# Two modulation vectors of the second layer, streamed behind the second pair of FFNs instead of the first FFN

## The chip, the cores and the metric

The kernel runs on one core of a Trainium2 chip. A core has a tensor engine for matrix products (TensorE, "PE" in the profile; its weight loads are "PEld"), a vector engine (VectorE, "DVE"), an activation engine (ScalarE, "ACT"), a general engine (GpSimd, "POOL") and a queue that issues transfers (SyncE, "SP"). Each runs its own list of instructions in order, and they wait for one another by semaphores. Sixteen DMA engines carry the transfers between the main memory and the core's own memory. The metric is the device time of one execution in microseconds (us).

## What is computed

Two layers of a diffusion backbone in 32-bit floats, on 256 latent tokens and 256 context tokens of 1024 features. Each layer is an FFN, a mixer (attention in the first layer, a short convolution in the second) and another FFN. Every such part is modulated by vectors that come from the conditioning vector `c`: nine vectors of 1024 numbers for each layer, one product of `silu(c)` with a 1024 x 9216 matrix.

```python
m = (s_c @ ada_w[i] + ada_b[i]).reshape(B, N_MOD, 1, D)
x = half_step_ffn(x, m[:, 0], m[:, 1], m[:, 2], ...)   # shift, scale, gate
hx = modulate(x, m[:, 3], m[:, 4])
x = post_norm_update(x, y_lat, m[:, 5], ...)
x = half_step_ffn(x, m[:, 6], m[:, 7], m[:, 8], ...)
```

An FFN is `(silu(a) * u) @ w_out` with `a, u` the halves of `h @ w_in`, 1024 to 2 x 2816 and 2816 to 1024. The change concerns vectors 2 and 3 of the second layer: the gate of its first FFN and the shift of its convolution.

## The kernel before

**Stages.** The kernel has three phases. The first (`ph0`, 0 to some 400 us) holds the first layer's first FFN for latent and context tokens together. The second (`ph1`, to some 600 us) is the attention. The third (`ph2`) is, from latent tokens alone, the first layer's second FFN, `ffn(..., 0, 1, ...)`, the second layer's first FFN, `ffn(..., 1, 0, ...)`, the convolution mixer and the last FFN. The text calls the first two of these the second pair of FFNs.

**Matrix products.** Every 32-bit factor is split in a high and a low part: ScalarE copies the raw tile to the high part (L216), VectorE subtracts it from the raw tile for the low part (L219). A product is then three matmuls: high by high (L170), low by high (L171), high by low (L173). A weight unit (`wunit`) is 256 rows by 512 columns, one or two loads from SP (L211), two ScalarE instructions and two VectorE instructions (`w1h`, `w1l` for the first matrix, `w2h`, `w2l` for the second). The low parts lie in five buffers and two further ones in `ph2`.

**Ticks.** TensorE's order is written out by hand. After each group of six matmuls the generator yields and `tick()` is called. An FFN in `ph2` has 88 ticks in the first matrix (11 panels, each of four units for two token tiles; panels 0 and 1 together take 16 ticks, each later panel 8) and 44 in the second. The first 5 units of the second matrix are used for the first token tile alone, one per tick; elsewhere a unit serves two ticks.

**Background stream.** Modulation vectors are computed beside the FFNs. `stream` is a generator of single steps. A step loads one slice of 128 rows of `ada_w` for a vector (L316, 128 x 1024, 512 KB, tile `ar`, three buffers) and multiplies an earlier one by its column of `silu(c)` into an accumulator (L305 for the first slice of a vector, L307 for the others; two VectorE instructions of 512 columns each, tile `acc`, two buffers). Eight slices make a vector. `tick()` takes steps at a rate per tick that `set_background` sets; in `ph2` the rate is `ADA_SLOWEST` and the first step comes after a hold of four ticks. The accumulations are queued behind the last gate product (`gate_ins`) and the last weight split.

**How a vector is finished.** The accumulator still holds 128 partial sums for each column. In `ph0` TensorE sums them by 32-row matmuls against `ones` (L342), VectorE adds the bias, and SP stores the rows to the scratch tensor `scr`. In `ph2` (`on_pool`) it is done by `sum_up`: GpSimd waits for the last gate product (`warm`, L350), reduces over the partitions (L356), and adds the result by a DMA of its own to `scr`, where the bias was put at the start of the phase (L357), with a small instruction behind (L359). `sum_up` is called behind the panels `SUM_AT = (2, 4, 6, 7, 8)`, by `need` at the end of the first matrix, and in the convolution. `need(n)` also runs steps at once until `n` vectors are streamed.

**Other work on the same engines.** VectorE and ScalarE also do the gate products (`sil`, L511 and L512), the splits of the transposed gates (`gh`, `gl`, L118 and L119), the layer norms between FFNs (`x`, L446, with `rs` on GpSimd, L435 and L436) and the folded columns of the next modulation (`gcol`, L399 to L402). DMA transposes of the gates (L519) are issued by SP.

Of the kernel before, what the change touches and what calls it, by code (L numbers as in the profile page):

```python
# [19 lines left out]
D = 1024  # L20
# [12 lines left out]
WB = (4, 5, 5)  # L33
PB = {"mm": 3, "at": 3, "tp": 2}
W_EARLY = 40
ADA_SLOW, ADA_FAST, ADA_SLOWEST = 3, 0.6, 0.13
KT_IDLE = 6
BIAS_AT = 24
ADA_LATE = 20
# [31 lines left out]
HOLD = 4  # L71
# [4 lines left out]
def backbone_kernel(  # L76
# [7 lines left out]
    sync = nc.sync  # L84
# [20 lines left out]
    def act(dt=F32, s="a"):  # L105
        return ap.tile([P, 512], dt, tag="act", name=nm(s))
# [10 lines left out]
    def split(src, hi, lo):  # L117
        a = nc.scalar.activation(hi, src, AF.Copy)  # L118
        return a, nc.vector.tensor_tensor(out=lo, in0=src, in1=hi.bitcast(F32), op=ALU.subtract)  # L119
# [20 lines left out]
    def settle():  # L140
        while waiting:
            waiting[0].get()

    def bg_step():
        with tc.high_priority(offset=-ada_late[0]):
            if next(background[0], 0) == 0:
                background[0] = None
# [10 lines left out]
    def set_background(gen, rate, hold=0):  # L158

        background[:] = [gen, rate, -rate * hold]  # L160
# [115 lines left out]
    scr = [tc.dram_tile([2, 9 * D], F32, name=f"scr{i}") for i in range(2)]  # L276
# [72 lines left out]
    def sum_up():  # L349
        mark = [nc.gpsimd.tensor_tensor(out=warm, in0=g[0:1, 0:1], in1=lnc[0:1, 0:1], op=ALU.add)  # L350
                for g in last_gate[:len(sums)]]
        while sums:
            (l, m, v), a = sums.pop(0)
            red = hp.tile([P, D], F32, tag="red", name=nm("red"))
            with queued(mark):
                nc.gpsimd.partition_all_reduce(red, a, P, ReduceOp.add)  # L356
            nc.gpsimd.dma_start(scr[l][v:v + 1, m * D:(m + 1) * D], red[0:1], accum_op=ALU.add)  # L357
            if not sums:
                nc.gpsimd.tensor_tensor(out=warm, in0=red[0:1, 0:1], in1=lnc[0:1, 0:1], op=ALU.add)  # L359
# [3 lines left out]
    def need(n):  # L363
        while made[0] < n:
            bg_step()
        sum_up()

    def stream(*groups):
        for g in groups:
            yield from ada(g)  # L370
            made[0] += 1
            if made[0] == ADA_SLOW:
                background[1] = ADA_FAST
# [101 lines left out]
    def lead_in(np):  # L475

        r = range(KU)
        o = [(0, 0, u) for u in r] + [(0, 1, u) for u in r[:2]] + [(1, 0, u) for u in r] + [(1, 1, u) for u in r[:2]]
        o += [(t, 1, u) for u in r[2:] for t in range(2)]
        return o + [(t, p, u) for p in range(2, np) for u in r for t in range(2)]  # L480

    def panels(cols, w, hTs, order, done, s, own=()):


        units, banks = {(0, u): x for u, x in enumerate(own)}, {}
        for t, p, u in order:
            if (p, u) not in units:
                with ExitStack() as st:
                    for i in fence if p == 1 else first_mv if own and p == 0 else ():
                        st.enter_context(tc.issue_after(i))  # L490
                    units[p, u] = wpair(w, u, *cols[p], s)
            if (t, p) not in banks:
                banks[t, p] = mmb(s, t)
            hi, lo = units[p, u]
            mmu(banks[t, p], [(*hsl(hTs[t], UK * u + i), hi[:, i], lo[:, i]) for i in range(UK)], u == 0, u == KU - 1)
            if u == KU - 1:
                done(p, t, banks.pop((t, p)))
            yield
            tick()

    def run(gen):
        for _ in gen:
            pass
# [39 lines left out]
    def order_skew(nu):  # L543

        u = [(n, i) for n in range(2) for i in range(nu)]
        o = []
        for i in range(len(u) + LEAD):
            if i < len(u):
                o.append((0, *u[i]))
            if i >= LEAD:  # L550
                o.append((1, *u[i - LEAD]))
        return o

    def order_last(nu):

        return order_skew(nu)[:-TAIL] + [(1, 1, u, c, c + 256) for c in (0, 256) for u in range(nu - TAIL, nu)]

    def order_late(nu, halved=False):


        e = nu - 1
        banks = ((0, 0), (0, 1), (1, 0))
        o = [(t, n, u) for t, n in banks for u in range(e - 1)] + [(t, n, e - 1) for t, n in banks]
        if halved:
            o += [(t, n, (e, i)) for i in range(UK) for t, n in banks]
        else:
            o += [(t, n, e) for t, n in banks]
        return o + [(1, 1, u) for u in range(nu)]
# [182 lines left out]
    for q, (k0, n) in enumerate(steps):  # L751
        nxt = start_step(*steps[q + 1]) if q < 4 else iter(())
        for g in range(6 * n):
# [7 lines left out]
            else:  # L761
# [3 lines left out]
    sync.dma_start(rope, rope_tab.rearrange("(t p) a b -> p t a b", p=P))  # L765
    w_early[0] = W_EARLY
    set_background(stream([(0, 2, 0), (0, 2, 1)], [(0, 3, 0), (0, 3, 1)], [(0, 4, 0), (0, 4, 1)],
                          [(0, 5, 0), (0, 6, 0)], [(0, 7, 0), (0, 8, 0)], [(1, 0, 0), (1, 1, 0)],
                          [(1, 2, 0), (1, 3, 0)]), 0.45)
    ada_late[0] = 0  # L770
    stats, gates, hTs = {}, [], {}
    GB = None
# [94 lines left out]
    def lhs_T(tl):  # L867
        def f(k, t):
            s = (k % 2) * 256 + t * P
            g = tl[k // 2]  # L870
            hi, lo = g.get() if isinstance(g, Late) else g
            return hi[:, s:s + P], lo[:, s:s + P]
        return f

    def ffn(hTs, later, l, j, i, gm, nxt, own=(), vectors=0):
        def finish(p, ps):
            hi, lo = act(F32R, "gh"), act(F32R, "gl")
            split(ps, hi, lo)
            return hi, lo

        done, gT = gated(AF.Silu, finish, "gT", BY_DMA)

        def done2(p, t, bk):
            done(p, t, bk)
            if t == 1:
                if p == 1:
                    later()
                if p in SUM_AT:
                    sum_up()

        run(panels([(p * 256, FF + p * 256) for p in range(NP)], ffn_w_in[l, j], hTs, lead_in(NP), done2, "w1", own))
        need(vectors)
        g, hTs, later = sub_end(ffn_w_out[l, j], lhs_T(gT), 2 * NP, l, i, gm, 0.5, nxt, "w2",
                                order_skew(NP) if nxt else order_last(NP))
        run(g)
        return hTs, later
# [263 lines left out]
    hTs, later = box  # L1160
    phase = tc.tile_pool(name="ph2", bufs=1)
    hp = phase.__enter__()
    on_pool[0] = True
    sync.dma_start(scr[1][0, 4 * D:9 * D].rearrange("(a b) -> a b", a=16), ada_b[1, 4 * D:9 * D].rearrange("(a b) -> a b", a=16))
    ext[0] = 2

    v0 = made[0]
    set_background(stream(*([(1, m, 0)] for m in range(4, 8))), ADA_SLOWEST, HOLD)
    hTs, later = ffn(hTs, later, 0, 1, 2, 8, (1, 0), own)

    hTs, later = ffn(hTs, later, 1, 0, 0, 2, (1, 3), (), v0 + 1)


    srow = cp.tile([P, P], F32, tag="row", name="srow")
# [33 lines left out]
    def done(p, t, bk):  # L1208
        if p >= 2:
            cdone(p, t, bk)  # L1210
            if t == 1:
                sum_up()
            return
        b = sp.tile([P, 512], F32, tag="s2", bufs=S2, name=nm("bs"))
        nc.scalar.activation(b, bk, AF.Copy)
        bs[p, t] = b
        last_gate[:] = [b]
        if p == t == 1:
            sum_up()
        if t == 1:  # L1220
            for j in range(2):
                def rest(j=j):
                    ps = tpb("bT")
                    for i in range(2):
                        for t in range(2):
                            nc.tensor.transpose(ps[:, i * 256 + t * P:i * 256 + (t + 1) * P],
                                                bs[p, t][:, (2 * j + i) * P:(2 * j + i + 1) * P], ident)
                    b = act(F32, "bT")
                    nc.scalar.activation(b, ps, AF.Copy)
                    return b  # L1230
                bT[2 * p + j] = Late(G_LAG, rest)
            if p == 1:
                later()

    cols = [(0, 256), (512, 768)] + [(D + n * 256, 2 * D + n * 256) for n in range(4)]
    run(panels(cols, w, hTs, lead_in(6), done, "wc"))
    need(v0 + 4)
    g, hTs, later = sub_end(sc_w_out[0], lhs_T(yT), KC, 1, 1, 5, 1.0, (1, 6), "wo", order_late(KU))
    run(g)
    set_background(stream([(1, 8, 0)]), 0.15)  # L1240
    ffn(hTs, later, 1, 1, 2, 8, None, (), v0 + 5)
    settle()
    phase.__exit__(None, None, None)

# [51 lines left out]
```

## Time and profile before

| what | value |
|---|---|
| median of 3 runs | 1245.14 us (1244.8 to 1246.18) |
| the profiled execution, whole | 1246.53 us |
| its span, first to last instruction | 1244.7 us |
| granted TensorE clock | 0.998 of full |
| slices loaded for vectors (`ar` at L316) | 128 of 512 KB |
| accumulations, L305 and L307 | 38 of 482 ns and 266 of 747 ns |
| matmuls against `ones` (L342) | 56 records, 7 groups, 97.7 to 362.2 us |
| all-reduces on GpSimd (L356) | 5 of 6.1 to 6.5 us, 722.2 to 1154.0 us |

A page of the profile gives, for one execution, each engine's busy time and the groups of instructions with their mean duration and the idle time ahead of them. A table by stage gives the busy time of each engine with its count of instructions in a stretch of the span. A timeline gives the instructions of an engine in order, and for the idle time before one, in brackets, what ended it. A name such as `w1l<-w1r,w1h` says what is written and what is read.

### The profile page before, as it was taken

The page shows a single profiled execution, that of the slowest core. Times are in us where ns is not written, and L with a number is a line of the kernel's source. Part 1 is how long each engine was busy: PE and PEld are TensorE (multiplying, and loading weights), DVE is VectorE, ACT ScalarE, POOL GpSimd, SP SyncE. Part 2 cuts the span into 40 slices and gives each one's busy share as a digit, 9 for nine tenths or more (in the row PEclk, how much of TensorE's full clock was granted, in tenths as well). Part 3 has the DMA queues.
Part 4 walks back from the last instruction along what each step waited for, and adds up shares of the span by engine and source line. Part 5 has one row for each costly group of instructions (what it writes and reads, how often), then busy time and mean ns, then how long its engine had stood idle before and what let it go on. Part 6 is the DMA issues. An engine that isn't in the chain of part 4 may idle for free.

```text
span 1244.7 us, 17236 instructions
## 1 busy us (share of the span) xinstructions
PE 1225.9 (98%) x5794; PEld 995.3 (80%) x5794; DVE 965.2 (78%) x1675; ACT 643.7 (52%) x1233; POOL 81.6 (7%) x93
## 2 busy tenths in 40 slices
PE   8999999999999999999999999999999999999997
PEld 5787778778778878777788888888888887888886
DVE  3698987888878867888877677878867798768746
ACT  2433132321325566687777635668645644678631
POOL 0000000000001011120000020020200110000200
PEclk9999999999999999999999999999999999999999
DMA  9986679778852654554899957879886765799851
GB/s 294 305 249 228 177 235 298 259 253 289 285 187 68 179 116 95 121 111 128 264 296 311 269 202 242 231 231 324 246 286 225 220 220 153 204 279 277 245 186 68
DMA packets 232304, 275.67 MB, mean 221 GB/s; under 512 B 59622, under 2 KB 178910, under 8 KB 232216
## 3 DMA queue, kind: packets, MB, share of 16 engines
q1 hardware_dynamic: 232020, 274.54, 73.0%
q8 instruction: 45, 0.74, 0.2%
q14 instruction: 43, 0.35, 0.1%
q0 software_dynamic: 160, 0.02, 0.1%
q10 hardware_dynamic: 36, 0.02, 0.0%
HBM read 265.27 MB, written 2.20 MB: 215 GB/s over the span
## 4 chain that ended last, share of the span: by engine, by line
PE 90%; DVE 4%; DMA 3%; ACT 2%; issue 1%; SPq 0%; POOL 0%; DVEq 0%; ACTq 0%
PE f L729 19%; PE w L170 17%; PE w L171 17%; PE w L173 17%; PE wkv L170 3%; PE wkv L171 2%; PE wkv L173 2%; DMA ar<-in_ada_w_dram 1%; PE wc L170 1%; PE wc L171 1%; PE wc L173 1%; PE S L1026 1%; PE o L1064 1%; PE hT L454 1%; PE PT L1051 1%
## 5 line engine op out<-in xcount | busy, mean ns | idle before, releaser
L219 DVE TENSOR_TENSOR w1l<-w1r,w1h 128x512 fp32r<-128x512 f32 (+1 forms) x352 | 232.0, 704 | 44.5 <-ACT w1h L216 43.6
L216 ACT ACTIVATE w1h<-w1r 128x512 fp32r<-128x512 f32 (+1 forms) x352 | 198.2, 617 | 112.0 <-DMA w1r<-in_ffn_w_in_dram 40.8
L170 PE MATMUL w<-w1h,hTh 128*128 128x512 f32 x528 | 206.3, 391 | 1.2 <-ACT hTh L118 1.2
L171 PE MATMUL w<-w1l,hTh 128*128 128x512 f32 x528 | 205.6, 389 | 0.0
L307 DVE SCALAR_TENSOR_TENSOR acc<-ar,cst,acc 128x512 f32<-128x512 f32 x266 | 186.6, 747 | 12.3 <-DMA ar<-in_ada_w_dram 11.9
L170 PE MATMUL w<-w2h,gh 128*128 128x512 f32 (+1 forms) x446 | 173.3, 389 | 0.0
L171 PE MATMUL w<-w2l,gh 128*128 128x512 f32 (+1 forms) x446 | 172.2, 387 | 0.0
L216 ACT ACTIVATE w2h<-w2r 128x512 fp32r<-128x512 f32 x176 | 101.3, 624 | 135.5 <-PE w L173 95.0
L173 PE MATMUL w<-w1h,hTl 128*128 128x512 f32 x528 | 162.6, 389 | 0.0
L219 DVE TENSOR_TENSOR w2l<-w2r,w2h 128x512 fp32r<-128x512 f32 x176 | 117.7, 710 | 57.6 <-ACT w2h L216 56.7
L173 PE MATMUL w<-w2h,gl 128*128 128x512 f32 (+1 forms) x446 | 136.1, 386 | 0.0
L729 PE MATMUL f<-h0h,w1h 128*128 128x512 f32 x352 | 132.4, 392 | 1.9 <-ACT w1h L216 1.5
L729 PE MATMUL f<-h0l,w1h 128*128 128x512 f32 x352 | 133.0, 391 | 0.0
L729 PE MATMUL f<-h0h,w1l 128*128 128x512 f32 x352 | 132.8, 390 | 0.0
L170 PEld LDWEIGHTS w<-w1h,hTh 128*128 128x128 f32 x528 | 99.1, 188 | 22.5 <-ACT hTh L118 2.1
L173 PEld LDWEIGHTS w<-w1h,hTl 128*128 128x128 f32 x528 | 99.0, 188 | 20.9 <-DVE hTl L119 0.4
L171 PEld LDWEIGHTS w<-w1l,hTh 128*128 128x128 f32 x528 | 99.2, 188 | 20.6 <-DVE w1l L219 0.3
L170 PEld LDWEIGHTS w<-w2h,gh 128*128 128x128 f32 x446 | 83.8, 188 | 19.2 <-issue 1.7
L171 PEld LDWEIGHTS w<-w2l,gh 128*128 128x128 f32 x446 | 83.8, 188 | 16.9 <-DVE w2l L219 0.3
L173 PEld LDWEIGHTS w<-w2h,gl 128*128 128x128 f32 x446 | 83.3, 188 | 17.1
L729 PEld LDWEIGHTS f<-h0h,w1h 128*128 128x128 f32 x352 | 65.7, 188 | 19.5 <-issue 3.4
L729 PEld LDWEIGHTS f<-h0l,w1h 128*128 128x128 f32 x352 | 65.6, 188 | 14.2 <-issue 0.8
(197 smaller groups left out, 1763.6 us busy)
## 6 DMA issues: line engine op xcount, KB each, us to landing
w1r<-in_ffn_w_in_dram SPq DMA_DIRECT2D x340, 256.0 KB
ar<-in_ada_w_dram SPq DMA_DIRECT2D x128, 512.0 KB
w2r<-in_ffn_w_out_dram SPq DMA_DIRECT2D x88, 512.0 KB
ar<-in_ada_w_dram SPq DMA_DIRECT2D x32, 256.0 KB
wkvr<-in_na_w_qkv_dram SPq DMA_DIRECT2D x32, 256.0 KB
wcr<-in_sc_w_in_dram SPq DMA_DIRECT2D x32, 256.0 KB
wqr<-in_na_w_qkv_dram SPq DMA_DIRECT2D x8, 512.0 KB
wor<-in_na_w_out_dram SPq DMA_DIRECT2D x8, 512.0 KB
```

Source lines behind the costliest of these rows:

```text
L170: nc.tensor.matmul(ps, lh, rh, start=first and i == 0, stop=False)
L171: nc.tensor.matmul(ps, lh, rl, start=False, stop=False)
L173: nc.tensor.matmul(ps, ll, rh, start=False, stop=last and i == n - 1)
L216: last_split[:] = [nc.scalar.activation(hi[:, a:a + m // W_HI], raw[:, a:a + m // W_HI], AF.Copy)]
L219: last_lo[:] = [nc.vector.tensor_tensor(out=lo[:, a:b], in0=raw[:, a:b], in1=hi[:, a:b].bitcast(F32), op=ALU.subtract)]
L307: nc.vector.scalar_tensor_tensor(out=a, in0=src, scalar=sc, in1=a, op0=ALU.mult, op1=ALU.add)
L454: nc.tensor.transpose(ps[:, k * P:(k + 1) * P], z[h][:, k * P:(k + 1) * P], ident)
L729: nc.tensor.matmul(ps, w, hT0[k][part == 1], start=(k == part == 0), stop=(k == KC - 1 and part == 1))
L1026: nc.tensor.matmul(banks[i], (qh, ql, qh)[f][ps, qs], (kh, kh, kl)[f][ps, :], start=f == 0, stop=f == 2)
L1051: nc.tensor.transpose(pt[:, k * P:(k + 1) * P], pr[:, k * P:(k + 1) * P], ident)
L1064: nc.tensor.matmul(ps, v[k][:, s], p[:, k], start=k == part == 0, stop=part == 1 and k == 3)
```

## The change

The first stream ends with vectors 0 and 1 of the second layer; vectors 2 and 3 go to the head of the second stream, which so has six vectors instead of four. Its rate goes from 0.13 to 0.21 steps per tick. The bias of seven vectors instead of five is put into `scr` at the start of the phase. The counts that `need` waits for are relative to `v0`, the count of groups streamed earlier, and grow by two for the two vectors more.

```diff
-ADA_SLOW, ADA_FAST, ADA_SLOWEST = 3, 0.6, 0.13
+ADA_SLOW, ADA_FAST, ADA_SLOWEST = 3, 0.6, 0.21
...
-                          [(0, 5, 0), (0, 6, 0)], [(0, 7, 0), (0, 8, 0)], [(1, 0, 0), (1, 1, 0)],
-                          [(1, 2, 0), (1, 3, 0)]), 0.45)
+                          [(0, 5, 0), (0, 6, 0)], [(0, 7, 0), (0, 8, 0)], [(1, 0, 0), (1, 1, 0)]), 0.45)
...
-    sync.dma_start(scr[1][0, 4 * D:9 * D].rearrange("(a b) -> a b", a=16), ada_b[1, 4 * D:9 * D].rearrange("(a b) -> a b", a=16))
+    sync.dma_start(scr[1][0, 2 * D:9 * D].rearrange("(a b) -> a b", a=16), ada_b[1, 2 * D:9 * D].rearrange("(a b) -> a b", a=16))
...
-    set_background(stream(*([(1, m, 0)] for m in range(4, 8))), ADA_SLOWEST, HOLD)
+    set_background(stream(*([(1, m, 0)] for m in range(2, 8))), ADA_SLOWEST, HOLD)
...
-    hTs, later = ffn(hTs, later, 1, 0, 0, 2, (1, 3), (), v0 + 1)
+    hTs, later = ffn(hTs, later, 1, 0, 0, 2, (1, 3), (), v0 + 3)
...
-    need(v0 + 4)
+    need(v0 + 6)
...
-    ffn(hTs, later, 1, 1, 2, 8, None, (), v0 + 5)
+    ffn(hTs, later, 1, 1, 2, 8, None, (), v0 + 7)
```

## The prediction

> **What bounds the kernel now.** I read the page's busy shares first, then the table by stage (busy time and instructions of each engine in a stretch, granted clock, share of the 16 DMA engines, GB/s), since a share over the whole span hides which stage has room.
>
> ```profile
> PE 1225.9 (98%) x5794; PEld 995.3 (80%) x5794; DVE 965.2 (78%) x1675; ACT 643.7 (52%) x1233; POOL 81.6 (7%) x93
> 48.00:362.00 314.00, 314.00 (x1404) 254.24 (x1402) 268.18 (x429) 96.14 (x168) 0.00 (x0) 1.00 0.77 248
> 525.00:600.00 75.00, 71.11 (x400) 55.65 (x401) 63.92 (x135) 59.09 (x128) 11.88 (x16) 1.00 0.54 137
> 600.00:715.00 115.00, 115.00 (x511) 95.06 (x510) 87.06 (x149) 83.52 (x155) 0.00 (x0) 1.00 0.97 284
> 715.00:777.00 62.00, 62.00 (x280) 50.82 (x279) 46.72 (x74) 27.92 (x53) 9.17 (x6) 1.00 0.66 220
> 777.00:898.00 121.00, 120.77 (x538) 99.48 (x537) 98.37 (x157) 86.85 (x160) 16.78 (x9) 1.00 0.91 259
> 898.00:960.00 62.00, 62.00 (x280) 51.12 (x279) 45.06 (x76) 27.69 (x52) 1.30 (x3) 1.00 0.79 259
> 960.00:1055.00 95.00, 93.50 (x435) 76.52 (x433) 80.05 (x139) 52.25 (x103) 10.20 (x8) 1.00 0.63 197
> ```
>
> TensorE bounds every stage. In the first FFN (48 to 362) it is never idle, though VectorE is busy 85% there. In the two FFNs of the change (600 to 960) it is idle for 0.23 us in all. So work taken from VectorE, SP or the DMA engines in the first FFN frees no TensorE time, and work added to the later FFNs costs nothing until a weight comes late. What counts is TensorE's own work that goes, and how far VectorE runs ahead of TensorE where work arrives.
>
> **What is removed.** Two vectors leave the first stream: 16 slices (16 `ar` loads of 512 KB, 32 VectorE instructions), two bias loads, one VectorE add, two stores to `scr`, and four 32-row matmuls against `ones` (L342). Only the matmuls are on TensorE. The last group's eight records stand between two matmul streams:
>
> ```profile
> 361.60 0.39 PE L729 MATMUL f<-h0h,w1l 128*128 128x512 f32 x1
> 361.82 0.39 PE L729 MATMUL f<-h0l,w1h 128*128 128x512 f32 x1
> 362.14 1.06 PE L342 MATMUL ada<-acc,ones 128*32 128x512 f32 x8
> 363.14 0.50 PE L170 MATMUL w<-w2h,gh 128*128 128x512 f32 x1
> ```
>
> From 361.82 to 363.14 are 1.32 us where two neighbouring matmuls are 0.23 apart, so the group costs 1.1 us: **-1.1 us**. The rest lies beside a TensorE without idle time: nothing. The attention stage's 3.9 us of idle time (75 - 71.11) begin some 160 us after the stream's end; I take no gain, and keep 3.9 as the bound of one.
>
> **What is added.** 16 slices more go into the streams behind the second FFN pair, and two more sums on GpSimd. A tick is six matmuls, 1.36 us. Loads come at 0.21 per tick for 0.13, so 0.08 per tick more: 7 in the 88 ticks of the first matrix, 3.5 in the 44 of the second. Step n falls on tick 4 + n/0.21; the accumulation lags one step, so vector j (from 0) is complete at step 8j + 9: ticks 47, 85, 123, 161, 199, 237, where four stood at 73, 135, 196, 258. Sums are taken behind panels 2, 4, 6, 7, 8 and at the end of the first matrix (ticks 24, 40, 56, 64, 72, 88 of an FFN of 132). So vectors 2 to 7 are summed at ticks 56, 88, 156, 172, 204 and in the convolution; before it was 88, 156, 204 and the convolution. **New are tick 56 (first FFN of the pair) and tick 172 (second, behind panel 4).** The second comes 16 ticks behind a sum that exists. `need(v0 + 3)` at tick 220 asks for 40 steps and finds 45, so it forces nothing.
>
> What a sum does to VectorE is in its rows and GpSimd's (start, duration, instruction):
>
> ```profile
> 820.16 0.63 POOL L350 TENSOR_TENSOR warm<-sil,lnc 1x1 f32<-1x1 f32 x1 [38.29 <-DVE sil L512]
> 827.48 6.13 POOL L356 PARTITION_ALL_REDUCE red<-acc  x1 [6.69 <-issue]
> 842.33 0.18 POOL L359 TENSOR_TENSOR warm<-red,lnc 1x1 f32<-1x1 f32 x1 [7.42 <-issue]
> 880.37 0.29 POOL L350 TENSOR_TENSOR warm<-sil,lnc 1x1 f32<-1x1 f32 x1 [37.86 <-DVE sil L512]
> 954.19 0.52 POOL L435 TENSOR_TENSOR rs<-mv,lnc 128x1 f32<-128x1 f32 x1 [50.63 <-DVE mv L433]
> 820.00 1.41 DVE L307 SCALAR_TENSOR_TENSOR acc<-ar,cst,acc 128x512 f32<-128x512 f32 x2
> 824.77 1.29 DVE L219 TENSOR_TENSOR w1l<-w1r,w1h 128x512 fp32r<-128x512 f32 x2
> 827.52 5.63 DVE L219 TENSOR_TENSOR w1l<-w1r,w1h 128x512 fp32r<-128x512 f32 x2 [1.47 <-ACT w1h L216]
> 836.12 1.29 DVE L219 TENSOR_TENSOR w1l<-w1r,w1h 128x512 fp32r<-128x512 f32 x2
> 843.36 0.42 DVE L512 TENSOR_TENSOR sil<-sil,w 128x256 f32<-128x256 f32 x1 [0.97 <-ACT sil L511]
> ```
>
> The pair of `w1l` beside the all-reduce takes 5.63 us where others take 1.29: VectorE is held for **4.3 us**. GpSimd itself is taken for 22 us (820.16 to 842.5); behind the new sum stands `rs` of the layer norm, not wanted before 954, so nothing waits there. With two accumulators, vector 4's first write (tick 166, at the earliest 777 + 34 x 1.36 = 823) waits for the all-reduce of vector 2 to end at 833.6, most of it while VectorE is held anyway; the rest is in the upper bound below. How much it can spare is read from the instructions on `w1l`, counted from 766, ahead of this FFN's first (columns: TensorE, weight loads, VectorE). A unit is two on VectorE and four on TensorE.
>
> ```profile
> 766.00:827.00 61.00, 28.02 (x72) 13.52 (x72) 26.94 (x42) 1.00 0.81 236
> 766.00:833.00 67.00, 31.45 (x81) 15.30 (x82) 32.41 (x44) 1.00 0.81 239
> 766.00:838.00 72.00, 34.24 (x88) 16.63 (x89) 34.10 (x47) 1.00 0.79 232
> 766.00:850.00 84.00, 41.24 (x106) 19.91 (x106) 41.52 (x59) 1.00 0.84 239
> 766.00:882.00 116.00, 59.49 (x153) 28.86 (x154) 59.00 (x86) 1.00 0.92 263
> ```
>
> At 827 VectorE has begun 21 units, TensorE 18: 3 ahead, 8 us. At 838 TensorE is through 22, and unit 23 (the pair after the 44 begun by 833, done at 836.12 + 1.29 = 837.4) is there 0.6 us ahead. So **one sum eats the lead down to 0.6 us**, and it comes back to 4.75 units (43 - 38.25) by 882: some 3.5 units of 2.72 us in 44 us, 0.22 us per us.
>
> A further slice costs VectorE two L307, 1.33 us back to back. 0.08 per tick make 0.078 us per us, and the regained lead falls to 0.14 if nothing hides them. These rows of the stage (busy, mean ns, idle before it) say what could:
>
> ```profile
> L219 DVE TENSOR_TENSOR w1l<-w1r,w1h 128x512 fp32r<-128x512 f32 x80 | 55.4, 739 | 9.5 <-ACT w1h L216 9.4
> L512 DVE TENSOR_TENSOR sil<-sil,w 128x256 f32<-128x256 f32 x20 | 8.2, 417 | 8.0 <-ACT sil L511 8.0
> ```
>
> The 9.5 us ahead of `w1l` can take work in; the 8.0 ahead of `sil` hardly, since ScalarE waits there for VectorE's `sil` in turn. I take half as hidden: 0.18 us per us. The terms:
> - Sum at tick 156: the half-hidden slices since 785 (2.5 of 1.33 us) take 1.7 from the 0.6 left: stall **1.0** (0 to 2.7).
> - Sum at tick 172: its first instruction waits for panel 4's gate (843.36) and, behind the other on GpSimd, for 842.33; the all-reduce follows 7.3 us later, near 851. The lead has regained 0.18 x 13 = 2.3. It takes 4.3 by the row above, some 6 by the fall of the lead at the first sum: stall **3.0** (0.7 to 4.2).
> - Sum at tick 204: 32 us give back 5.8, it takes 4.3 to 6, and the second matrix's first five units are used at one per tick: **1.0** (0 to 4).
> - Sums in the pair's first FFN: at tick 56 the lead stands; the one at tick 88 meets a smaller lead, see below: **0.4** (0 to 3).
> - Turn from FFN to FFN, below: **0.6** (0 to 1.3).
>
> ```profile
> 782.52 1.11 PE L454 MATMUL hT<-ident,x 128*128 128x128 f32 x8 [0.23 <-DVE x L446]
> 775.47 1.33 DVE acc L307 x2
> 722.19 6.13 POOL L356 PARTITION_ALL_REDUCE red<-acc  x1 [5.74 <-issue]
> 723.90 2.85 DVE L400 SCALAR_TENSOR_TENSOR gcol<-gcol 128x8 f32<-128x8 f32 x1
> 650.00:675.00 25.00, 25.00 (x112) 20.70 (x111) 20.07 (x35) 20.69 (x39) 0.00 (x0) 1.00 1.13 327
> ```
>
> At the turn TensorE already waits 0.23 us, and the chain of waits runs through an accumulation (775.47); 16 us of it hold 0.9 more, at 1.33 each at most. At 722 the sum holds VectorE (2.85 us for a 128x8 instruction) while TensorE uses a unit per tick; before, VectorE was as far ahead as its buffers allow. The loads: 7 more `ar` are 3.7 MB on 32.7 (115 us at 284 GB/s), 316 GB/s, under the 327 seen from 650 to 675. SP issues them in one queue with the weights, so a late `ar` buffer also holds weights; I put that into the high end.
>
> [...]
>
> **The sum.** 1.0 + 3.0 + 1.0 + 0.4 + 0.6 - 1.1 = +4.9 us. The profiled execution took 1246.53 (span 1244.7, 1.8 around it), so it would take 1251.4; it lies 1.4 above the median of 1245.14, so the forecast is **1250.0**.
>
> **The rivals.**
> 1. Not slower: the idle 9.5 us hide all slices, and stalls are no more than the lead. It decides at the second of the two close sums: lead over 5 us at 850 (before: 2.5 to 3 units, 59/2 - 106/4, so it needs nearly what was there plus what the sum at 156 no longer takes). Then 1245.1 - 1.1 = 1244, up to 1247 with the turn's wait. For it: no stall in either FFN today. Against: 0.6 us left after a single sum.
> 2. Nothing is hidden, and the loads run late: the upper ends, 2.7 + 4.2 + 4 + 3 + 1.3 - 1.1 = +14, some 1259, or 1254 and over. For it: DMA share 0.97 and 0.91; against: VectorE's idle time.
> 3. Faster: the attention stage gains from the emptied first FFN, or the turn into the convolution from a stream that ends 21 ticks earlier (237 for 258). Bounds: 3.9 and 1.5 (95 - 93.50); with the 1.1, 1239 at best, likelier 1242. Against: TensorE is busy all of 898 to 960.
> 4. That the change doesn't stream the vectors where it says: the counts above leave no room.
>
> **How the numbers follow.** Forecast (1247.6 to 1254) 0.45, rival 1 0.33, rival 2 0.17, rival 3 0.05. About 0.2% (2.5 us) is what a measurement of this kernel can tell from no change. Slower 0.45 + 0.17 = 0.62, same 0.33, faster 0.05. The range, 1243.8 to 1257, leaves out rival 3 and the worst of rival 2.
>
> **What would show it.** Right: six L342 groups; all-reduces in the second FFN near 828, 851 and 890, with TensorE idle behind each and released by VectorE's `w1l` or `w2l`; idle time of 777 to 898 grown from 0.2 to 5 us. Wrong: TensorE still full there (rival 1), `w1h` waiting for its loads (rival 2), or less idle time from 525 to 600 (rival 3).

## The result, and the profile after

The changed kernel takes **1263.11 us** (median of 4, 1261.02 to 1264.08) against 1244.97 beside it: **1.0142 times as long, 95% interval 1.0124 to 1.0159**. It was forecast at 1250.0, range 1243.8 to 1257: the direction was right, the loss three to four times too small. The profiled execution is the fastest of the four, 1261.02 us with a span of 1258.9, 14.2 more than the span of before. Counted from the first matmul of a part to the first of the next, those 14.2 us lie here:

| part | before, us | after, us | difference |
|---|---|---|---|
| up to the first FFN of the pair | 593.1 | 589.8 | -3.3 |
| first FFN, first matrix | 121.6 | 122.3 | +0.7 |
| first FFN, second matrix | 61.7 | 67.8 | **+6.1** |
| second FFN, first matrix | 121.8 | 132.7 | **+10.9** |
| second FFN, second matrix | 61.6 | 61.6 | 0.0 |
| convolution to the end | 284.9 | 284.7 | -0.2 |

Of the first row, 1.4 us lie ahead of the first matmul with a second-matrix weight (116.56 before, 115.13 after) and are chance: over the kernels of this study it starts at 114.2 to 117.0. Behind it 1.2 us are the matmuls that went (see the account of the prediction) and 0.6 the attention.

The table by stage after, for the stretches shown of before (columns as there; the second FFN now lies some 4 to 14 us later, so its last rows are shifted):

```profile
48.00:362.00 314.00, 314.00 (x1403) 254.35 (x1402) 248.34 (x399) 96.13 (x167) 0.00 (x0) 1.00 0.69 222
600.00:715.00 115.00, 114.67 (x508) 94.60 (x507) 93.12 (x155) 79.18 (x144) 9.63 (x4) 1.00 0.97 293
715.00:777.00 62.00, 57.66 (x252) 46.66 (x251) 50.48 (x80) 24.96 (x46) 9.91 (x6) 0.97 0.76 267
777.00:898.00 121.00, 118.62 (x522) 95.98 (x520) 96.78 (x157) 80.08 (x149) 17.76 (x11) 1.00 0.88 262
898.00:960.00 62.00, 57.02 (x245) 47.04 (x246) 48.19 (x76) 29.68 (x54) 7.63 (x3) 0.94 0.80 270
```

The first FFN lost 20 us of VectorE's work (268.18 to 248.34) and TensorE is as busy in it as before: nothing is gained there. In the pair TensorE now has idle time, and the granted clock falls below 1. From 777 to 898 the DMA engines carry hardly more than before (262 for 259 GB/s), though 0.08 slices per tick were added. They are not fuller; what they should carry comes late.

TensorE's timeline after, with the longest idle times of the pair in brackets and what ended them, and the matmuls behind the last:

```profile
734.54 0.79 PE L171 MATMUL w<-w2l,gh 128*128 128x512 f32 x1 [2.62 <-DVE w2l L219]
861.54 0.50 PE L171 MATMUL w<-w1l,hTh 128*128 128x512 f32 x1 [0.68 <-DVE w1l L219]
865.79 0.50 PE L171 MATMUL w<-w1l,hTh 128*128 128x512 f32 x1 [1.08 <-DVE w1l L219]
902.98 1.11 PE L537 MATMUL gT<-ident,sil 128*128 128x128 f32 x4 [5.12 <-DVE sil L512]
904.32 0.63 PE L171 MATMUL w<-w1l,hTh 128*128 128x512 f32 x1
904.74 0.63 PE L170 MATMUL w<-w1h,hTh 128*128 128x512 f32 x1
```

The two longest stalls cost twice. Behind the 5.12 us neighbouring matmuls start 0.42 us apart (904.32 to 904.74) where 0.23 is usual. The granted clock is halved from 733.95 to 737.36 and from 901.20 to 908.03. The stage table of these places, for TensorE alone (busy time and matmuls, granted clock, share of the DMA engines, GB/s):

```profile
730.54:733.95 3.41, 1.38 (x7) 1.00 0.00 0
733.95:737.36 3.41, 2.82 (x7) 0.50 0.05 1
897.79:901.20 3.41, 0.07 (x1) 1.00 1.21 294
901.20:904.62 3.42, 1.64 (x6) 0.50 1.05 386
904.62:908.03 3.41, 3.41 (x9) 0.50 1.04 401
```

TensorE works 2.82 and 5.05 us at the half clock. With 0.20 us lost in every 0.43, that is some 1.3 and 2.4 us more, an estimate.

The sums, on GpSimd's timeline, and VectorE's instructions around the one of 728:

```profile
728.14 6.13 POOL L356 PARTITION_ALL_REDUCE red<-acc  x1 [9.08 <-issue]
828.30 6.13 POOL L356 PARTITION_ALL_REDUCE red<-acc  x1 [6.23 <-issue]
856.40 6.13 POOL L356 PARTITION_ALL_REDUCE red<-acc  x1 [6.57 <-issue]
903.46 6.45 POOL L356 PARTITION_ALL_REDUCE red<-acc  x1 [8.25 <-issue]
```

```profile
728.16 5.72 DVE L307 SCALAR_TENSOR_TENSOR acc<-ar,cst,acc 128x512 f32<-128x512 f32 x2
733.80 2.48 DVE L219 TENSOR_TENSOR w2l<-w2r,w2h 128x512 fp32r<-128x512 f32 x4
```

In the first FFN a sum does stop TensorE: it holds two accumulations for 5.72 us, and the `w2l` behind them ends the stall of 734.54. In the second FFN the sums stand about where they were forecast, but the rows don't fit them. Between the sums of 828 and 856 nothing stops TensorE. The longest stall, up to 902.98, ends before the all-reduce of 903.46 has begun. What ScalarE waited for there, before and after:

```profile
ACT w1h L216 <- DMA w1r<-in_ffn_w_in_dram: 8.8, 9, 2.4
```

```profile
ACT w1h L216 <- DMA w1r<-in_ffn_w_in_dram: 28.7, 20, 3.6
```

The columns are total, times and longest in us, from 777 to 900. The weights come late: 28.7 us for 8.8. At the longest stall itself ScalarE is at work, but behind: it splits weights until 901.59, the second matrix's too, and only then makes the `sil` for which TensorE has waited since 897.86.

### The profile page after: what moved, and what is told of

It is laid out like the page before. It is cut to its first block, busy times and chain, and to the rows that moved or that the text cites. A ratio compares the mean times of both kernels' runs of the same rounds, so it can differ in the third digit from the quotient of the medians.

```text
span 1258.9 us, 17236 instructions
## 1 busy us (share of the span) xinstructions
PE 1229.8 (98%) x5786; PEld 999.5 (79%) x5786; DVE 966.6 (77%) x1674; ACT 645.4 (51%) x1233; POOL 103.1 (8%) x101
## 4 chain that ended last, share of the span: by engine, by line
PE 75%; DVE 9%; DMA 7%; ACT 5%; issue 3%; SPq 1%; POOL 0%; DVEq 0%; ACTq 0%
PE f L729 19%; PE w L171 12%; PE w L170 12%; PE w L173 12%; DMA w1r<-in_ffn_w_in_dram 5%; DVE w1l L219 4%; PE wkv L170 2%; PE wkv L171 2%; PE wkv L173 2%; PE wc L170 2%; PE wc L173 2%; PE wc L171 2%; ACT w1h L216 1%; DVE acc L307 1%; PE S L1025 1%
## 5 line engine op out<-in xcount | busy, mean ns | idle before, releaser
L307 DVE SCALAR_TENSOR_TENSOR acc<-ar,cst,acc 128x512 f32<-128x512 f32 x266 | 198.1, 790 | 9.8 <-DMA ar<-in_ada_w_dram 9.8
L219 DVE TENSOR_TENSOR w2l<-w2r,w2h 128x512 fp32r<-128x512 f32 x176 | 113.5, 687 | 55.9 <-ACT w2h L216 54.9
L729 PEld LDWEIGHTS f<-h0l,w1h 128*128 128x128 f32 x352 | 65.6, 188 | 14.2 <-issue 0.8
```

The source lines that it names most:

```text
L219: last_lo[:] = [nc.vector.tensor_tensor(out=lo[:, a:b], in0=raw[:, a:b], in1=hi[:, a:b].bitcast(F32), op=ALU.subtract)]
L307: nc.vector.scalar_tensor_tensor(out=a, in0=src, scalar=sc, in1=a, op0=ALU.mult, op1=ALU.add)
L729: nc.tensor.matmul(ps, w, hT0[k][part == 1], start=(k == part == 0), stop=(k == KC - 1 and part == 1))
```

## The experiments

All times are medians; the ratio is to the kernel before on the same chip, with its 95% interval. The last three columns are the first FFN's second matrix, the second FFN's first matrix and the convolution's first product in the profiled execution, counted as above. The kernels e1 to e3, e6, e7, e10, e13, e14 and e17 leave work out or read an old tile, and stand here for their times alone.

| kernel | us | ratio | FFN 1, second | FFN 2, first | conv. |
|---|---|---|---|---|---|
| before | 1244.97 | 1 | 61.7 | 121.8 | 70.2 |
| after | 1263.11 | 1.0124 to 1.0159 | 67.8 | 132.7 | 69.6 |
| e1_no_loads | 1256.04 | 1.0078 to 1.0108 | 62.6 | 134.6 | 69.6 |
| e2_no_acc | 1257.41 | 1.0088 to 1.0118 | 63.0 | 132.6 | 69.6 |
| e3_no_sums | 1256.30 | 1.0078 to 1.0114 | 62.5 | 132.5 | 69.6 |
| e4_sums_only | 1245.85 | 0.9997 to 1.0016 | 61.8 | 121.8 | 69.6 |
| e5_rate_only | 1261.29 | 1.0100 to 1.0148 | 67.0 | 122.3 | 69.6 |
| e6_ffn2_no_loads | 1251.97 | 1.0042 to 1.0076 | 67.7 | 121.8 | 71.1 |
| e7_ffn2_no_acc | 1249.77 | 1.0021 to 1.0043 | 67.1 | 121.5 | 69.6 |
| e8_sum_later | 1264.70 | 1.0137 to 1.0178 | 67.2 | 131.7 | 69.9 |
| e9_transposes_act | 1286.37 | 1.0290 to 1.0347 | 63.6 | 137.4 | 70.6 |
| e10_small_loads | 1255.53 | 1.0062 to 1.0092 | 66.7 | 121.8 | 70.3 |
| e11_rate19 | 1272.13 | 1.0195 to 1.0226 | 62.4 | 144.2 | 69.6 |
| e12_rate17 | 1249.96 | 1.0025 to 1.0050 | 61.6 | 124.6 | 73.3 |
| e13_no_sum172 | 1258.77 | 1.0094 to 1.0164 | 66.9 | 129.5 | 71.0 |
| e14_no_sums_ffn2 | 1260.03 | 1.0096 to 1.0136 | 65.9 | 131.9 | 70.7 |
| e15_rate16 | 1263.83 | 1.0132 to 1.0162 | 61.6 | 123.4 | 70.1 |
| e16_two_rates | 1252.13 | 1.0033 to 1.0068 | 62.4 | 122.4 | 73.1 |
| e17_free_transposes | 1251.76 | 1.0044 to 1.0094 | 66.7 | 121.8 | 69.6 |
| e18_two_rates_b | 1270.84 | 1.0180 to 1.0214 | 61.6 | 148.7 | 70.8 |

### Which part of the added work costs: the first FFN

Three kernels leave out one part for vectors 2 and 3: their loads, their accumulations, or their sums. (Of an edit, the lines that matter are shown.)

```diff
+                if not (on_pool[0] and m in (2, 3) and k):
                     w = hp.tile([P, D], F32, tag="ar", bufs=3, name=nm("ar"))
                     sync.dma_start(w, ada_w[l, k * P:(k + 1) * P, m * D:(m + 1) * D])
```

> The changed kernel (1263 us), in which vectors 2 and 3 of the second layer load their first slice only and use it eight times: 14 of the 16 added loads of 512 KB are gone, accumulations and sums stay. If the loads make the weights late (theory L), 1246 to 1250 us and ScalarE's wait for w1r falls back near the 9 us that it had between 777 and 898. If VectorE's added instructions (theory V) or the held VectorE during the sums (theory S) do it, 1258 to 1263 us.

```diff
-                    if vec[:2] != (l, m):
+                    if vec[:2] != (l, m) or on_pool[0] and m in (2, 3) and k:
```

> The changed kernel, in which vectors 2 and 3 accumulate their first slice only: 28 VectorE instructions of 0.75 us (21 us in all) are gone, the loads and the sums stay. Theory V: 1246 to 1252 us. Theories L and S: 1258 us or more.

```diff
-            if on_pool[0] and k == KC - 1:
+            if on_pool[0] and k == KC - 1 and m not in (2, 3):
```

> The changed kernel without the all-reduces and adds to the scratch rows of vectors 2 and 3 (these vectors stay at their bias): GpSimd has four sums in the second FFN pair and the convolution, as before the change, at ticks 156, 172, 204 and in the convolution. Theory S: the stall of 2.6 us at the turn to the second matrix of the first of the two FFNs goes and some 5 us with its slow clock; in the second FFN the sums stay, so 1255 to 1258 us. Theories L and V: 1261 us or more.

Each of the three takes the loss of the second matrix from 6.1 us to 0.8 to 1.3, and none touches the second FFN, where other vectors are streamed. So no part alone is the price; the stall needs all three. Loads and accumulations thin the lead (how far the splits run ahead of TensorE), and the sum, which now falls 16.0 us into the matrix (728.14) instead of 7.5 (722.19) and beside two accumulations, finds nothing left. (SP issues nothing from 725.95 to 736.85 either: a load of finished rows, `mrow`, at the head of its queue waits for this sum's result. It did not make the stall: ScalarE had split the weights of the late unit at 729.01, and VectorE was held until 733.88.)

Next came the kernel before with each half of the change alone: two sums more (of a tile no longer used, behind panels 6 and 4, ticks 56 and 172, each as two all-reduces of 512 columns and 3.3 to 3.8 us), or the rate of 0.21 without the two vectors.

```diff
+                if (l, j, p) in ((0, 1, 6), (1, 0, 4)):
+                    sums.append((None, extra[0]))
```

> The kernel before (1245 us) with two more sums at the places of the changed kernel's new ones, tick 56 and tick 172: each is two all-reduces over 512 columns of a constant tile, into a scratch row that nothing reads. Loads, rate and accumulations are those of before. Theory S: 1248 to 1250 us, a stall behind the sum at tick 172. Theories L and V: 1245 to 1246 us.

```diff
-ADA_SLOW, ADA_FAST, ADA_SLOWEST = 3, 0.6, 0.13
+ADA_SLOW, ADA_FAST, ADA_SLOWEST = 3, 0.6, 0.21
```

> The kernel before (two vectors still in the first FFN) with the second stream at 0.21 steps per tick instead of 0.13: the same 32 loads and sums, in 156 ticks instead of 250. The FFN up to tick 132 then has the loads, accumulations and sums of the changed kernel (ticks 56 and 88), and the second FFN has its two close sums (156 and 172) but no accumulation behind tick 161. If the rate near the close sums is the cause, the first FFN's 6 us stay and the second FFN's 11 us go: 1250 to 1253 us. If the two close sums alone stall the second FFN: 1258 to 1262 us. If nothing but the count of vectors matters: 1245 us.

Sums at the forecast places cost nothing at the rate of before (0.9997 to 1.0016, 121.8 us). The rate alone costs nearly what the whole change costs, without a vector moved: 1261.29 us. That is the time expected of two close sums in the second FFN, but it is lost elsewhere: the second FFN, where the stream is nearly done, keeps 122.3, and the first takes 131.9 us in its first matrix for 121.6, 67.0 in its second.

The 131.9 is not the rate's alone: the changed kernel has the same rate there and takes 122.3. The orders of SP's, ScalarE's and VectorE's instructions differ there in one load, which in this kernel stands in SP's queue 26 us ahead of the matrix's end:

```profile
690.12 0.58 SPq L211 DMA_DIRECT2D w1r<-in_ffn_w_in_dram  x1
696.72 0.30 SPq L393 DMA_DIRECT2D mrow<-scr  x1
```

It waits for a sum's result, SP issues nothing from 690.70 to 696.72, and the matrix's longest stall, 7.87 us, ends at 713.28. That this load makes the difference is read from the rows; no run takes it away.

### The second FFN

The same cuts for vectors 5 and 6, then loads of 2 KB in place of 512 KB with as many issues:

```diff
+                if not (on_pool[0] and m in (5, 6) and k):
```

> The changed kernel, in which vectors 5 and 6, streamed in the second FFN (ticks 127 to 204), load their first slice only and use it eight times: 14 loads go, accumulations and sums stay. Theory L (late weight loads): the second FFN's first matrix, 132.7 us for 121.8 before, falls to 122 to 125, in all 1252 to 1255 us. Theory V (VectorE's time): it stays over 130, 1261 us or more.

```diff
+                    if vec[:2] != (l, m) or on_pool[0] and m in (5, 6) and k:
```

> The changed kernel, in which vectors 5 and 6 accumulate their first slice only: 28 VectorE instructions of 0.75 us in the second FFN are gone, the loads and sums stay. Theory V: the second FFN's first matrix falls to 122 to 125 us, in all 1252 to 1255. Theory L: over 130 us, 1261 or more.

```diff
+                if on_pool[0] and m in (5, 6) and k:
+                    tiny = sm.tile([P, 4], F32, tag="tiny", bufs=3, name=nm("tiny"))
+                    sync.dma_start(tiny, ada_w[l, k * P:(k + 1) * P, m * D:m * D + 4])
```

> The changed kernel, in which seven of the eight slices of vectors 5 and 6 are replaced by loads of four columns (2 KB instead of 512 KB) into a small tile; the first slice is used eight times, accumulations and sums stay. SP issues as many loads as in the changed kernel. If the bytes on the DMA engines make the weights late, it is like the run without these loads: second FFN's first matrix 122 us, 1252 us in all. If SP's issues and their waits do it, the first matrix stays over 128 us and the whole over 1257.

All three bring 121.5 to 121.8 us back, with the sums left in. SP's issues are not it, the bytes are; and the accumulations as much. The table by stage of the kernel without these accumulations shows that the bytes alone are carried well:

```profile
777.00:898.00 121.00, 120.50 (x536) 99.21 (x535) 93.59 (x143) 87.96 (x168) 24.46 (x13) 1.00 1.00 299
```

299 GB/s at a share of 1.00, and TensorE hardly idle; the changed kernel stalls at 262 and 0.88. So full DMA engines are not what makes the weights late. In steps of 10 us they have room around the stalls of 861 and 865 (857 to 867: 0.71, 228 GB/s; before 1.12, 312). From 877 up to the longest stall they are full (1.06 to 1.10), but so are those of the kernel without these accumulations from 837 to 877 (1.05 to 1.14), where TensorE does not stop.

Three kernels ask for the sums: one takes a later place for the second, one leaves out vector 5's, one those of vectors 4, 5 and 6.

```diff
-SUM_AT = (2, 4, 6, 7, 8)
+SUM_AT = (2, 6, 7, 8)
```

> The changed kernel with no sum behind panel 4: the sum of vector 5 moves from tick 172 to tick 188 (panel 6), everything is computed. If the sum that follows 16 ticks behind another is what empties the lead (theory S, the forecast's largest term), its 3 us and the clock's share go: 1256 to 1259 us. If loads or accumulations keep the lead down, 1261 us or more.

```diff
-            if on_pool[0] and k == KC - 1:
+            if on_pool[0] and k == KC - 1 and m != 5:
```

> The changed kernel without the sum of vector 5 (the one at tick 172 of the second FFN; its loads and accumulations stay, and the modulation vector made from it is not the sum). If the sum at 172 is what stops TensorE, as the prediction had it, the first matrix of the second FFN goes from 132.7 us to 122 to 126 and the time to 1252 to 1256. If loads and accumulations thin the lead by themselves and any sum or late load then stops TensorE, that matrix stays above 129 and the time above 1259.

```diff
+            if on_pool[0] and k == KC - 1 and m not in (4, 5, 6):
```

> The changed kernel without the sums of vectors 4, 5 and 6 (loads and accumulations stay; these three modulation vectors are not summed). If sums are a necessary part, the first matrix of the second FFN falls to 122 to 123 us and the time to 1251 to 1253, as it did in the first FFN without the sums of vectors 2 and 3. If loads and accumulations alone empty the lead, it stays at 127 or more and the time at 1256 or more.

The matrix takes 131.7, 129.5 and 131.9 us. **At this rate the sums are not needed for the loss of the second FFN.** Without any of the three TensorE still waits (its timeline):

```profile
876.32 0.50 PE L171 MATMUL w<-w1l,hTh 128*128 128x512 f32 x1 [1.09 <-DVE w1l L219]
903.09 1.12 PE L537 MATMUL gT<-ident,sil 128*128 128x128 f32 x4 [6.15 <-DVE sil L512]
```

### The loop that makes the loads late

SP's and ScalarE's timelines of the changed kernel, around 850:

```profile
841.36 1.70 SPq L211 DMA_DIRECT2D w1r<-in_ffn_w_in_dram  x3
847.56 1.20 SPq L519 DMA_TRANSPOSE halT<-hal  x1
848.86 1.98 SPq L211 DMA_DIRECT2D w1r<-in_ffn_w_in_dram  x2
850.93 1.19 SPq L519 DMA_TRANSPOSE halT<-hal  x1
852.21 0.53 SPq L316 DMA_DIRECT2D ar<-in_ada_w_dram  x1
852.79 1.99 SPq L211 DMA_DIRECT2D w1r<-in_ffn_w_in_dram  x4
```

```profile
843.24 1.15 ACT L216 ACTIVATE w1h<-w1r 128x512 fp32r<-128x512 f32 x2 [2.94 <-DMA w1r<-in_ffn_w_in_dram]
...
846.91 0.63 ACT L518 ACTIVATE hal<-sil 128x512 uint16<-128x512 uint16 x1 [0.90 <-DVE sil L512]
...
848.81 0.61 ACT L518 ACTIVATE hal<-sil 128x512 uint16<-128x512 uint16 x1
...
858.04 1.15 ACT L216 ACTIVATE w1h<-w1r 128x512 fp32r<-128x512 f32 x2 [3.23 <-DMA w1r<-in_ffn_w_in_dram]
```

ScalarE waits 2.94 us for a load, then does the splits of two units and a `sil`; only behind them stands `hal` (846.91), the copy of the gate. SP had its transpose of that copy next in its queue and issues nothing from 843.06 to 847.56. The weight loads stand behind the transpose: from 843.06 to 852.79, 9.7 us, two are issued, one unit, where TensorE uses 3.6 (2.72 us each). So ScalarE waits again, 3.23 us at 858.04. A late load makes the next one late. The view of SP's waits from 777 to 900 sums it up, first before, then after:

```profile
SPq L519 <- ACT w1h L216: 17.7, 9, 5.3
```

```profile
SPq L519 <- ACT w1h L216: 24.6, 7, 6.5
...
SPq L519 <- ACT sil L511: 6.8, 3, 3.9
...
SPq L519 <- ACT gTw L524: 4.6, 3, 2.4
SPq L519 <- ACT hal L518: 3.9, 2, 2.9
SPq L316 <- DVE w1l L219: 1.3, 3, 0.6
```

The `ar` loads (L316) hold SP hardly at all; the transposes (L519) do: 23.9 us in all their rows before, 40.4 after. The same count over the second FFN's first matrix is 19 to 27 us in the kernels where that matrix takes up to 124.6 us and 36 to 45 where it takes 129.5 or more, leaving out the two with changed transposes below. Such a wait can be cause or effect. A first try gave them to ScalarE's queue:

```diff
-                sync.dma_start_transpose(part[p][:, :, t * P:(t + 1) * P], halves.rearrange("p s f -> p (s f)"))
+                nc.scalar.dma_start_transpose(part[p][:, :, t * P:(t + 1) * P], halves.rearrange("p s f -> p (s f)"))
```

> The changed kernel with the DMA transposes of the gates (L519) issued by ScalarE's queue instead of SP's; everything is computed. Theory Q (a transpose at the head of SP's queue waits for the gate on ScalarE and holds the weight loads behind it, so that loads, splits and gates fall behind together): the stalls of both FFNs go or shrink, 1246 to 1252 us, and ScalarE's wait for w1r between 777 and 900 falls under 10 us. Rival B (the 16 DMA engines do not carry the added bytes in time): 1260 us or more, and ScalarE's own time for the issues may add to it.

It was slower, and settles nothing: ScalarE waited for weights only 6.2 us from 777 to 900, but its own queue now had the issues (1.2 us each in SP's rows above), and every first matrix got longer, the last FFN's too (127.4 for 121.3). The second try leaves the transposes in SP's queue and takes the wait away (the edit also gives `hal` other buffers; the copies of the second FFN share one, which no transpose reads):

```diff
-                sync.dma_start_transpose(part[p][:, :, t * P:(t + 1) * P], halves.rearrange("p s f -> p (s f)"))
+                if where[0] != (1, 0):
+                    where[1] = halves
+                sync.dma_start_transpose(part[p][:, :, t * P:(t + 1) * P], where[1].rearrange("p s f -> p (s f)"))
```

> The changed kernel, with the DMA transposes of the second FFN reading a tile that was written in the FFN before, in place of ScalarE's fresh copies of the gates. The number and size of all instructions stay, the gates of that FFN are not transposed, and SP's queue no longer waits there for ScalarE's copies; the transposes are issued somewhat earlier. If the loop ScalarE - transposes - weight loads enlarges the loss, the first matrix of the second FFN goes from 132.7 us to 126 or less and the time to 1257 or less. If bytes and engine work make it without that loop, it stays at 130 or more and the time at 1260 or more. The first FFN keeps its 68 us in the second matrix either way.

**121.8 us**: the whole loss of the second FFN is gone, with all loads, accumulations and sums in place, while the first FFN keeps its loss (66.7 us). The table by stage and GpSimd's timeline of this kernel:

```profile
777.00:898.00 121.00, 120.64 (x542) 99.56 (x541) 107.55 (x168) 86.75 (x163) 22.62 (x12) 1.00 0.94 289
```

```profile
829.41 6.13 POOL L356 PARTITION_ALL_REDUCE red<-acc  x1 [9.37 <-issue]
853.52 6.31 POOL L356 PARTITION_ALL_REDUCE red<-acc  x1 [7.04 <-issue]
893.80 6.54 POOL L356 PARTITION_ALL_REDUCE red<-acc  x1 [7.54 <-issue]
```

The DMA engines carry 289 GB/s for 262, VectorE does 107.55 us for 96.78, and three sums, two of them 24 us apart, stop nobody. SP's waits from 777 to 900 are now for buffers that VectorE frees, and hardly at the transposes (here L522):

```profile
SPq L211 <- DVE w1l L219: 32.2, 26, 6.5
...
SPq L522 <- ACT w1h L216: 2.1, 2, 1.2
```

So neither the bytes nor the engines' work makes the loss without that wait. Two of this kernel's six executions took 1258.2 and 1259.5 us; no profile shows what cost them 7 us. Its transposes also stand earlier in SP's queue than those of the changed kernel, so the edit moves them besides freeing them.

### Other rates

The changed kernel at 0.19, 0.17 and 0.16 (one number each), then at two rates, which lower the stream in the first matrix of the two FFNs and raise it in the second (0.12 and 0.3; 0.16 and 0.32):

```diff
+        if nxt:
+            background[1] = 0.12
         run(panels([(p * 256, FF + p * 256) for p in range(NP)], ffn_w_in[l, j], hTs, lead_in(NP), done2, "w1", own))
         need(vectors)
+        if nxt:
+            background[1] = 0.3
```

> The changed kernel at 0.19 steps per tick, nearly the least at which five vectors are there at tick 220 (40 steps need 0.185); everything is computed. If the stalls grow with the added work step by step, a fourth of the 18 us goes: 1258 to 1260 us. If there is an edge below which the lead is regained, 1245 to 1250 us.

> The changed kernel at 0.17 steps per tick: by tick 220 it has 36 of the 40 steps that need asks for, and the missing ones are run at once at the end of the second FFN's first matrix; everything is computed. Half of the added rate, so 1254 us if the stalls grow step by step, 1245 to 1248 us if there is an edge, and up to 3 us more for the steps in a block.

> The changed kernel with a least rate of 0.16 in place of 0.21: 24% fewer loads and accumulations a tick, so the last of the 48 steps falls near tick 300. If the rate sets the loss, both stages come back to within 3 us of before (61.7 and 121.8 us) and the time is 1245 to 1251. If moving the two vectors costs by itself, the time stays above 1256.

> The changed kernel with a rate of 0.12 steps a tick in the first matrix of the two FFNs and 0.3 in the second. If what counts is that the first matrix leaves no room beside its own weight loads and transposes, the first matrix of each FFN takes 121 to 123 us, the second at most 65, and the time is 1244 to 1252. If the amount of work in the FFN counts wherever it is put, the second matrix takes the loss instead: 67 us or more there and a time of 1254 or more.

> As the kernel with two rates, but 0.16 in the first matrix and 0.32 in the second, so that vector 6 is complete at tick 217 and summed ahead of the second matrix, and only one sum is left in the convolution. If the pair of sums is what the convolution lost there (73.1 against 70.2 us), the convolution is back at 70 to 71 us. The first matrix of the second FFN, by the row of the kernel at 0.16, 123 to 125 us. Time 1246 to 1252; a first matrix above 128 would speak for a sharp edge between 0.12 and 0.16.

(The text on the first two, like the prediction, says that `need(v0 + 3)` wants 40 steps; it wants three vectors, some 25. It forces nothing either way.)

With the rate the first FFN's loss goes (61.6 us in the second matrix at 0.16 and 0.17). The second FFN doesn't follow the rate smoothly: 123.4, 124.6, 144.2 and 132.7 us at 0.16, 0.17, 0.19 and 0.21. At 0.19 the first FFN's first matrix loses 3.4 us (125.0), vector 3 misses the sum at tick 88, and in the second FFN two sums come back to back at 824.5 and 835.3 on the thinned lead. At 0.16 both FFNs are nearly whole, and the time is lost where it was not expected: vector 7 is finished too late, and TensorE waits in the middle of the convolution's output product for the load of the finished vector's rows:

```profile
1053.90 0.45 PE L397 MATMUL mcT<-ident,mrow 128*128 128x128 f32 x1 [14.36 <-DMA mrow<-scr]
```

The first pair of rates streams all six vectors with 62.4, 122.4 and 62.5 us in the pair's matrices, near before (61.7, 121.8, 61.6). So not the amount of work is dear, but its place. It loses 2.9 us in the convolution, where two sums meet (all-reduces at 995.37 and 1006.00). The second pair missed: the convolution is mended (70.8), but three sums fall on 33 us of the second FFN (818.51, 828.93, 851.16), and it takes 148.7 us. That is far from the 123.4 at the same rate there, where two sums stood 27 us apart. Of all kernels with the two vectors moved, none is faster than before.

## Why the prediction was right or wrong

- **Nothing gained in the first FFN but the matmuls, -1.1 us.** Right: TensorE is busy 314.00 of 314 us in both. From the first matmul with a second-matrix weight to the attention's first are 281.43 us before and 280.23 after, 1.2 us less. All 17 kernels with the shorter stream have 280.2 there, the three with the longer one 281.4.
- **The sum at tick 156, 1.0 us.** Not seen: no stall between the sums of 828 and 856.
- **The sum at tick 172, 3.0 us, the largest term.** Not what the loss is. Its sum came at 856 (forecast 851), and TensorE's two stalls behind it, 0.68 and 1.08 us, with slower steps beside them, make some 2.5 us. But two sums more cost nothing in the kernel before, and most of the loss is there without this sum (129.5 us, 3.2 less) and without any of the three (131.9, 0.8 less).
- **The sum at tick 204, 1.0 us (0 to 4).** Wrong cause: the 5.12 us and the halved pace behind them, some 7.5 us together, begin ahead of that sum, and come from late loads.
- **The sums at ticks 56 and 88, 0.4 us (0 to 3).** Right mechanism, mis-sized: a sum held VectorE for 5.7 us where the prediction had seen 2.85. Without both sums the second matrix takes 5.3 us less (62.5 for 67.8), beyond the upper end. The sum came later and beside accumulations, and the halved pace was not in the working.
- **The turn, 0.6 us.** Right: 0.98 us at 776.33 for 0.23 before.

The step that failed is the one that took the loads to be free. The prediction set 316 GB/s against a stretch of 327 and put "a late `ar` buffer also holds weights" into the high end. Bandwidth was enough (299 GB/s without loss), and `ar` buffers held SP for some 2 us; but SP was held by its transposes, which wait for ScalarE, which waits for the loads. That chain was in the profile of before, 17.7 us of waits of the same kind, and was not read. It made up the 10.9 us of the second FFN: without the transposes' wait they are gone.

For the same reason VectorE's 9.5 us of idle time ahead of `w1l` was room to hide work in only as long as the loads came in time. ScalarE ended it, and ScalarE was waiting for loads. With 0.08 slices per tick more that idle time grew; the row from 777 to 898 after:

```profile
L219 DVE TENSOR_TENSOR w1l<-w1r,w1h 128x512 fp32r<-128x512 f32 x81 | 57.5, 753 | 15.1 <-ACT w1h L216 14.8
```

In the kernel with free transposes, where the same work is hidden, it shrinks to 6.9 us. So the lead that the prediction worked out from VectorE's time alone was lost on the way from SP to ScalarE. Rival 2 had half of this, that the loads run late and `w1h` waits for them. But it saw a want of DMA bandwidth where the wait was in SP's queue, and its upper ends, summed to 1259, were still 4 us too low.

How the added loads and accumulations set the loop off together, and why either alone doesn't, is not shown by a run of its own. That a later VectorE makes `sil`, and so `hal`, later is read from the rows (0.90 us of wait ahead of the `hal` of 846.91); that the added bytes slow each load is the author's estimate, which no row shows. Why the same rate costs the first matrix of the first FFN only 0.7 us is open.

## What to carry to other kernels

Ask of each in-order queue what stands behind its longest wait: a transpose that waits for a result in the queue of the weight loads can turn one late load into a chain of them, and here did so with the DMA engines at a share of 0.71. Before you take a waiting engine's idle time as room, follow what it waits for to the end. Lead, not busy time, is what the background work used up here, and it did not go in proportion: at 0.17 the second FFN's first matrix lost 2.8 us, at 0.21 10.9, and at one and the same 0.16 it lost 1.6 or 26.9 by where the sums fell. And try a moved part in halves: the sums alone and the rate alone told in two runs that the largest term of the sum was not the loss.

## What was not expected of the hardware

The pace of TensorE after a stall. In the traces of this study, 13 stalls past the first 50 us lasted 2.0 to 3.1 us, and only ten of them are followed by a slower pace, with matmuls 0.42 to 0.43 us apart; all 16 longer ones are. One that is not, in the kernel without the second FFN's sums, and the stage table around it (TensorE alone, as above):

```profile
733.65 0.50 PE L171 MATMUL w<-w2l,gh 128*128 128x512 f32 x1 [3.02 <-DVE w2l L219]
```

```profile
729.14:732.56 3.42, 1.50 (x7) 1.00 0.10 37
732.56:735.97 3.41, 2.32 (x10) 1.00 0.02 5
```

The slower pace goes with the granted clock. In all 20 traces this changes only at steps of 3.41 us: in the changed kernel at 733.95, 737.36, 901.20 and 908.03, which are 1, 48 and 2 such steps apart. In these rows a fall goes with the idle time within one step, not with the length of a stall. The 2.62 us of the changed kernel put 2.03 us into one step, and the clock fell at its end; the 3.02 us above lie 1.92 in one step and 1.09 in the next, and it held. Between the kernels' starts and ends the clock fell 27 times, 26 of them behind a step with 2.01 to 3.41 us of idle time, and it fell behind every step at full clock that had as much. Only one step with less lost it, with 1.40 us, in the attention stage of the kernel with two sums more. Each fall lasts one to four steps; TensorE works 2.7 to 5.9 us of that at the half clock, which by the same estimate as above costs 1.3 to 2.8 us.

The all-reduce held VectorE for less than its own length, as forecast from before: an accumulation pair beside it took 5.72 us where others take 1.41, so 4.3 us for an all-reduce of 6.13.
